# Two layers of a streaming encoder in fp32: the MLP's up projection as seven block products for eight, and the down projection as a stage of its own

## The chip, the cores and the metric

One core of a Trainium2 chip. The number that counts is the device time of one execution in microseconds (us), median of several runs. A kernel of this size shows runs that lie within about 0.3% of each other.

## What is computed

Two layers on 1152 tokens (1024 of a prompt, 8 x 16 new ones of running streams), all in fp32. In each layer three kinds of attention (MLA, gated linear attention, chunk band attention) add to `x` through `w_out`; then comes the MLP, which is all that the change touches:

```
def _mlp(h, w_up, w_down):
    return jnp.square(jax.nn.relu(h @ w_up)) @ w_down
# x = x + _mlp(_rmsnorm(x, norm2), w_up, w_down)
# x: 1152 x 1024, w_up: 1024 x 4096, w_down: 4096 x 1024
```

A last RMSNorm gives `y`.

## The kernel before

`x` is held transposed: eight tiles `xs[c]` of 128 channels (partitions) by 1152 tokens. Tokens go in three groups of `G` = 384, which is the width of a matmul's moving operand and of a PSUM bank's used part. The kernel lets a scheduler order the instructions of each engine; the priorities in the code (`tc.high_priority`) and the order of the code are its input.

**Products of high and low parts.** An fp32 operand is split in two fp32r tiles: the high part is a ScalarE copy to fp32r, the low part a VectorE (or GpSimd) subtraction of that copy from the source. A product is then three matmuls: high x high, high x low, low x high. `wsplit` does it for weights: one DMA of 512 KB into `raw`, one ScalarE copy of 128x1024 (L146), one VectorE subtraction of 128x1024 (L135, in the helper `sub_l`). `mm_step` (L209) issues the three matmuls of one contraction chunk, and all matmuls carry the line of the helper `mm`, L57.

**Ahead of the MLP.** `out_last` (L1190) adds the last part of the output projection to `x`: per chunk and group nine matmuls and one VectorE add (L1200, `x<-z,xo`). `norm_group` (L194) makes `h` of one group: `inv_rms` gives the reciprocal root mean square in PSUM (`rb`), then per chunk one VectorE product `hf` (L199), one ScalarE copy and one subtraction. All `h` of a layer, high and low, stays in SBUF (48 tiles of the pool `h`).

**The MLP.** It runs over 16 blocks `fb` of 256 hidden rows. `up(f)` makes 128 hidden rows for all three groups: 8 contraction chunks x 3 matmuls x 3 groups = 72 matmuls of 384 columns. `u_evac` squares: ScalarE relu (L1225) and square (L1226), GpSimd product (L1227), VectorE subtraction, so that `u` is in SBUF in high and low parts. `down(fb, us)` multiplies these two chunks with `w_down` and adds each of the 24 results to `xs` on VectorE (L1253, `x<-z,x`): 8 x 3 x 6 = 144 matmuls of 384 columns and 24 adds. So the code alternates:

```
for fb in range(16):
    if 0 < fb < 15:
        nxt = up(2 * fb + 2)
    (down if fb < 15 else down_last)(fb, us)
    if fb < 15:
        us = [nxt, up(2 * fb + 3)]
```

The first three chunks of `up` run group by group behind the norm (`behind_norm`), the last `down` group by group ahead of the next norm (`down_last`). A layer has 32 x 72 = 2304 matmuls of up and 16 x 144 = 2304 of down. `u` never leaves SBUF. All DMAs of the kernel are issued by SyncE (SP), in one order.

Of the kernel before, what the change touches and what calls it, by code (L numbers as in the profile page):

```python
# [9 lines left out]
F32 = mybir.dt.float32  # L10
# [6 lines left out]
P = 128  # L17
DEPTH = 2
# [8 lines left out]
N_STREAM = 8  # L27
LEVELS = (32, 16, 8, 4, 2, 1)
# [6 lines left out]
# in-projection chunks of 128 columns  # L35
# [4 lines left out]
def body(ctx, tc, t):  # L40
    nc = tc.nc
    cpool = ctx.enter_context(tc.tile_pool(name="const", bufs=1))
    hpool = ctx.enter_context(tc.tile_pool(name="h", bufs=48))
    ppool = ctx.enter_context(tc.tile_pool(name="piece", bufs=8))
    wpool = ctx.enter_context(tc.tile_pool(name="wts", bufs=3))
# [20 lines left out]
    # chunks whose squares, and whose sums of squares, GpSimd makes  # L66
# [30 lines left out]
    def banks(**bufs):  # L97
        """a new cut of the eight banks"""
# [57 lines left out]
    def inv_rms(srcs, width, scale=1.0, heads=1, pool=SQ_POOL):  # L156
        """1 / root mean square over the partitions (of each head) of the given [P, G] views, in PSUM"""
        pt = bank("nm" if "nm" in pcur else "tp", "ms")
        accs = {}
        for i, c in enumerate(srcs):  # L160
            q = ppool.tile([P, G], F32, tag="q", name=nm("sq"), bufs=4)
# [9 lines left out]
        for i, q in enumerate(accs.values()):  # L171
            for j in range(3):
                mm(pt[:, j * heads:(j + 1) * heads], q[:, j * P:(j + 1) * P], onec if heads == 1 else hsel,
                   start=i == 0 and j == 0, stop=i == len(accs) - 1 and j == 2)
        n = 3 * heads
        v, r, w = (sm("rr", 6, 12)[:, :n] for _ in range(3))
        V.tensor_scalar(v, pt[:, :n], scale / width, EPS * scale, ALU.mult, ALU.add)
# [6 lines left out]
        # one row of it for all partitions  # L184
        pr = bank("nm" if "nm" in pcur else "pv", "rb")
        m = P // heads
        for j in range(3):
            for h in range(heads):
                c = j * heads + h
                mm(pr[h * m:(h + 1) * m, j * P:(j + 1) * P], r[:, c:c + 1].to_broadcast([P, m]), ident,  # L190
                   start=True, stop=True)
        return pr[:, :G]
# [16 lines left out]
    def mm_step(outs, w, r, first, last_):  # L209
        """one contraction chunk of all groups in outs; w, r: (high, low)"""  # L210
# [33 lines left out]
    for l in range(DEPTH):  # L244
# [47 lines left out]
        def behind_norm(ws, put):  # L292
            """three columns of products over all chunks, group by group behind the norm"""
# [11 lines left out]
        def dense(o, w, r, n):  # L305
            """a bank over n contraction chunks"""
# [51 lines left out]
        def drive(primary, pc, fc):  # L358
            """merge the primary stream with the dense one, in proportion to their costs"""
# [35 lines left out]
        def attention(unit_iter, ap, wmax, ny, lag):  # L395
            """units of one head and two query tiles; a unit gives scores(a), j0(a), nk(a), v(j), out(ps)"""
# [23 lines left out]
            def t_step(u, a, pr):  # L420
                if a == 0:
# [6 lines left out]
                    # blocks that one of the two query tiles does not see  # L428
# [66 lines left out]
        def v_split(dst, src):  # L495
            """src [P, n, 128] two heads of values -> dst [P, n, 4, 64]: high|low, low|high"""
# [76 lines left out]
        def ca_setup2(c, ap, box):  # L573
# [15 lines left out]
            # sample: scores of this pair of heads  # L589
# [43 lines left out]
        def sample_pt(pnew, pc, pn, sc):  # L633
            """P^T of the cached keys [128, stream, 96] and of the new keys (own stream only)"""
# [774 lines left out]
```

## Time and profile before

| what | value |
|---|---|
| median of 3 runs | 3263.82 us (3259.57 to 3268.15) |
| the profiled execution: span from first to last instruction | 3266.2 us |
| TensorE (PE) busy | 3137.7 us, 96% |
| VectorE (DVE) busy | 1834.2 us, 56% |
| ScalarE (ACT) busy | 1190.6 us, 36% |
| GpSimd (POOL) busy | 866.1 us, 27% |
| DMA | 237.67 MB, mean 73 GB/s |
| MLP of the first layer, first up matmul to last | 828.6 us to about 1634 us |
| MLP of the second layer, last down matmul | about 3245 us |

The execution's time other than its span is not listed apart; its span lies 2.4 us over the median of the runs and inside their range. The page shows, for each engine, busy time, a strip of 40 slices of the span (a digit is the busy share in tenths; a slice is 81.7 us), the chain of work that ended last, the costliest groups of instructions with their mean duration, and DMA issues with their time to landing. PEld is the weight load that each matmul has; it overlaps the matmuls. Matmuls overlap too, so what one costs in a dense stretch is the distance between starts and not its duration.

### The profile page before, as it was taken

What the parts mean: (1) busy time and instruction counts of PE and PEld (TensorE: products, weight loads), DVE (VectorE), ACT (ScalarE), POOL (GpSimd) and SP (SyncE); (2) the same over time, 40 slices, a digit from 0 to 9 for tenths busy, and PEclk for the clock granted to TensorE, in tenths of its full rate; (3) what the DMA queues carried; (4) which work ended last, traced back from release to release, by engine and by line L of the source; (5) the groups of instructions that cost most, each with busy time, mean ns of one, the idle gap of its engine ahead of it and who ended that gap; (6) DMA issues with size and microseconds to landing.
All of it is one profiled execution on the core that took longest, in us unless ns stands there. A gap on an engine that the chain in (4) does not pass through costs nothing.

```text
span 3266.2 us, 49236 instructions
## 1 busy us (share of the span) xinstructions
PE 3137.7 (96%) x18652; PEld 2982.4 (91%) x18652; DVE 1834.2 (56%) x3785; ACT 1190.6 (36%) x2781; POOL 866.1 (27%) x1122
## 2 busy tenths in 40 slices
PE   8999998998999999999999999889999999999998
PEld 7888887887999999999989888878889999999998
DVE  4554687885734434434555646978855443434436
ACT  4443454774311121111244434557743121111122
POOL 5221355443310010100242214654532010010112
PEclk9999999989999999999999999999999999999998
DMA  5232215224011111111143222142331111111111
GB/s 182 86 100 78 88 50 159 67 83 149 30 43 46 39 46 40 46 39 46 62 140 105 85 74 86 57 150 75 111 104 39 46 40 46 40 46 45 40 46 59
DMA packets 137612, 237.67 MB, mean 73 GB/s; under 512 B 16768, under 2 KB 105056, under 8 KB 137376
## 3 DMA queue, kind: packets, MB, share of 16 engines
q1 hardware_dynamic: 137376, 234.53, 22.3%
q8 instruction: 147, 2.41, 0.3%
q14 instruction: 89, 0.73, 0.1%
HBM read 178.64 MB, written 55.84 MB: 72 GB/s over the span
## 4 chain that ended last, share of the span: by engine, by line
PE 82%; DVE 9%; ACT 4%; issue 3%; DMA 1%; POOL 1%; SPq 0%; DVEq 0%; ACTq 0%; POOLq 0%
PE z L57 67%; PE s L57 4%; PE pv L57 3%; PE ptp L72 2%; PE rb L57 1%; DVE ga L743 1%; PE glao L57 1%; DVE mq L734 1%; PE lev L57 1%; DVE sbd L796 1%; ACT P L413 1%; DVE M L729 1%; PE ms L57 0%; DVE ng L408 0%; ACT PT L151 0%
## 5 line engine op out<-in xcount | busy, mean ns | idle before, releaser
L57 PE MATMUL z<-u,wdnh 128*128 128x384 f32 x3072 | 712.9, 334 | 0.1
L57 PEld LDWEIGHTS z<-u,wdnh 128*128 128x128 f32 x3072 | 548.6, 188 | 0.4 <-DVE u L135 0.4
L1253 DVE TENSOR_TENSOR x<-z,x 128x384 f32<-128x384 f32 x720 | 364.5, 551 | 288.0 <-PE z L57 288.0
L1227 POOL TENSOR_TENSOR relu<-relu 128x384 f32<-128x384 f32 x192 | 166.7, 895 | 1340.8 <-ACT u L1226 1336.1
L57 PE MATMUL z<-u,wdnl 128*128 128x384 f32 x1536 | 445.9, 334 | 0.0
L57 PE MATMUL z<-hH,wupl 128*128 128x384 f32 x1536 | 373.3, 334 | 0.0
L57 PE MATMUL z<-hL,wuph 128*128 128x384 f32 x1536 | 373.1, 334 | 0.0
L57 PE MATMUL z<-hH,wuph 128*128 128x384 f32 x1536 | 372.2, 334 | 0.0
L146 ACT ACTIVATE wdnh<-wdnr 128x1024 fp32r<-128x1024 f32 x64 | 68.0, 1062 | 686.4 <-PE z L57 686.4
L57 PEld LDWEIGHTS z<-u,wdnl 128*128 128x128 f32 x1536 | 282.3, 188 | 0.0
L57 PEld LDWEIGHTS z<-hH,wupl 128*128 128x128 f32 x1536 | 275.8, 188 | 0.0
L57 PEld LDWEIGHTS z<-hL,wuph 128*128 128x128 f32 x1536 | 275.8, 188 | 0.0
L57 PEld LDWEIGHTS z<-hH,wuph 128*128 128x128 f32 x1536 | 275.7, 188 | 0.0
L146 ACT ACTIVATE wuph<-wupr 128x1024 fp32r<-128x1024 f32 x64 | 68.0, 1062 | 514.6 <-PE z L57 512.6
L135 DVE TENSOR_TENSOR wdnl<-wdnr,wdnh 128x1024 fp32r<-128x1024 f32 x64 | 78.1, 1221 | 302.7 <-ACT wdnh L146 302.7
L135 DVE TENSOR_TENSOR wupl<-wupr,wuph 128x1024 fp32r<-128x1024 f32 x64 | 78.2, 1221 | 205.8 <-ACT wuph L146 205.8
L413 ACT ACTIVATE P<-s,ng 128x320 f32<-128x320 f32 (+5 forms) x288 | 157.4, 552 | 85.8 <-DVE ng L410 59.1
L135 DVE TENSOR_TENSOR u<-relu,u 128x384 fp32r<-128x384 f32 x192 | 148.9, 801 | 50.9 <-POOL relu L1227 50.9
L135 DVE TENSOR_TENSOR PT<-ptp,PT 128x512 fp32r<-128x512 f32 (+3 forms) x288 | 146.0, 518 | 52.6 <-ACT PT L151 44.3
L151 ACT ACTIVATE PT<-ptp 128x512 fp32r<-128x512 f32 (+3 forms) x288 | 127.3, 460 | 126.1 <-PE ptp L72 116.5
L72 PE MATMUL ptp<-ident,P 128*128 128x128 f32 x792 | 139.9, 283 | 15.2 <-DVE PT L135 12.0
L408 DVE TENSOR_REDUCE ng<-s 128x1 f32<-128x320 f32 (+5 forms) x288 | 146.7, 516 | 7.0 <-PE s L57 2.7
(416 smaller groups left out, 6447.5 us busy)
## 6 DMA issues: line engine op xcount, KB each, us to landing
wupr<-in_w_up_dram SPq DMA_DIRECT2D x64, 512.0 KB, 3.3
wdnr<-in_w_down_dram SPq DMA_DIRECT2D x64, 512.0 KB, 3.3
zs_dram<-z SPq DMA_DIRECT2D x102, 192.0 KB, 1.9
wo1r<-in_w_out_dram SPq DMA_DIRECT2D x48, 320.0 KB, 3.0
of<-os_dram SPq DMA_DIRECT2D x48, 192.0 KB, 3.5
xpart_dram<-xo SPq DMA_DIRECT2D x48, 192.0 KB, 1.9
xo<-xpart_dram SPq DMA_DIRECT2D x48, 192.0 KB, 3.5
cf<-zs_dram SPq DMA_DIRECT2D x36, 192.0 KB, 4.3
```

The costliest lines, as they stand in the source:

```text
L57: i = T.matmul(*a, **k).ins
L72: T.transpose(out, in_, idn)
L135: eng.tensor_tensor(lo, src, h.bitcast(F32), ALU.subtract)
L146: S.activation(h, raw, AF.Copy)
L151: S.activation(o, i, AF.Copy, scale=scale)
L408: V.tensor_reduce(ng[:, x:x + 1], sc[x][:, :hi - lo], AX.X, ALU.max, negate=True)
L413: S.activation(pr[:, lo:hi], sc[x][:, :hi - lo], AF.Exp, bias=ng[:, 0:1], accum_out=ss[:, x:x + 1])
L729: V.tensor_tensor(mv[:, :, 0, :], mv[:, :, 0, :], kv[:, :, 0, :], ALU.mult)
L734: (GP if h else V).tensor_tensor(q2[hr, h, :w // 2].rearrange("p (n s) -> p n s", s=s), mv[hr, :, 1, :], qv[hr, :, 1, :], ALU.mult)
L743: V.copy_predicated(o, mk.to_broadcast([P, 2 * nt, 64 // s, s]), src)
L1227: GP.tensor_tensor(r, r, r, ALU.mult)
L1253: V.tensor_tensor(x[:, gsl(g)], o, x[:, gsl(g)], ALU.add)
```

## The change

Up and down become two stages, with `u` in DRAM between them.

**Up.** Both operands of up are cut in 2 x 2 blocks: the weights of a pair of hidden chunks (2 x 128 hidden rows, contraction in two halves of four chunks) and `f` = the normed `x` (contraction halves, token blocks of `Q` = 288; half `h` of the tokens is two such blocks). A block product then takes seven products in place of eight (Winograd's form of Strassen). `up_pair(i, halves)` does a pair: it loads 2 x 512 KB, forms four sums of weights (`ws`, two on GpSimd, two on VectorE, 128x512), splits seven operands (`oh` on ScalarE, `ol` on VectorE, 128x512), issues 7 x 4 x 3 = 84 matmuls of 288 columns for each half of the tokens, and combines the results: per half one ScalarE copy, five VectorE adds, then relu and square of four blocks, two on VectorE alone, two on ScalarE and GpSimd, and four stores to `u` in DRAM. `f_blocks` and `f_sums` make, per half, for each of four j: four VectorE products `f`, three VectorE and one GpSimd difference, then seven splits into tiles `hc` (ScalarE copy, VectorE subtraction, 128x288). The order of the code: norm and `hc` of half 0; pairs 0 to 3 for half 0 with norm and `hc` of half 1 in between; pairs 4 to 15 for both halves; pairs 0 to 3 for half 1, whose weights are loaded, summed and split a second time.

**Down.** Eight blocks of 512 hidden rows (2, 3, ..., 7, 0, 1). `load_u` reads four chunks of `u` (128x1152 each) and splits them, `load_d` loads and splits weights, and `down` runs 12 matmuls of 384 columns into one bank and adds the result to `x`: 24 adds a block, 192 a layer. In the first block the addend is `xo`, read from a copy `xmid` of `x` in DRAM, since `xs` is given up during up for the tiles `hc` of half 1.

**Pools.** `wts` and `h` are closed ahead of the MLP (`base.close()`) and opened again behind it, so their memory serves the MLP's pools.

The diff of the MLP, cut (comments and docstrings go too):

```diff
+Q = NT // 4
+KH = KD // 2
+PRODUCTS = range(7)
...
-        for g in range(NG):
-            with tc.high_priority(offset=100):
-                norm_group(xs, sml[:, SM_N2:SM_N2 + 8], hs, g)
...
-        def u_evac(u, g, o):
-            uh, ul = u[g]
-            r = piece("relu")
-            S.activation(r, o, AF.Relu)
-            S.activation(uh, r, AF.Square)
-            GP.tensor_tensor(r, r, r, ALU.mult)
-            sub_l(V, ul, r, uh)
...
-        def up(f):
-            w = wsplit(t["w_up"][l, f], [KD, P], "wup")
-            u = new_u()
-            outs = list(enumerate(dense3()))
-            for k in range(KD):
-                mm_step(outs, (w[0][:, k, :], w[1][:, k, :]), hs[k], k == 0, k == KD - 1)
-            for g, o in outs:
-                u_evac(u, g, o)
-            return u
...
-        def down(fb, us):
-            for half in range(2):
-                w = wsplit(t["w_down"][l, fb, half], [2, 512], "wdn")
-                for m in range(4):
-                    outs = list(enumerate(dense3()))
-                    for k in range(2):
-                        mm_step(outs, (w[0][:, k, m * P:(m + 1) * P], w[1][:, k, m * P:(m + 1) * P]), us[k],
-                                k == 0, k == 1)
-                    x = xs[half * 4 + m]
-                    for g, o in outs:
-                        V.tensor_tensor(x[:, gsl(g)], o, x[:, gsl(g)], ALU.add)
...
+        base.close()
...
+        hc = [[[mp.tile([P, 1, Q], F32R, name=nm("hc")) for _ in range(2)] for _ in range(KH)] for _ in PRODUCTS]
...
+        def f_sums(f):
+            f11, f12, f21, f22 = f
+            t1, t2, t3, t4 = (e_tile("t") for _ in range(4))
+            V.tensor_tensor(t1, f12, f11, ALU.subtract)
+            GP.tensor_tensor(t3, f22, f12, ALU.subtract)
+            V.tensor_tensor(t2, f22, t1, ALU.subtract)
+            V.tensor_tensor(t4, f21, t2, ALU.subtract)
+            return f11, t2, t3, t1, f21, t4, f22
...
+        def up_pair(i, halves):
...
+                r = mp.tile([P, KD, P], F32, tag="wr", name=nm("wur"), bufs=3)
+                load(r, t["w_up"][l, 2 * i + c])
...
+            GP.tensor_tensor(s1, a21, a22, ALU.add)
+            V.tensor_tensor(s2, s1, a11, ALU.subtract)
+            GP.tensor_tensor(s3, a11, a21, ALU.subtract)
+            V.tensor_tensor(s4, a12, s2, ALU.subtract)
...
+            def prod(n, src, banks_, first, after):
+                wh = mp.tile([P, KH, P], F32R, tag="oh", name=nm("oh"), bufs=5)
+                wl = mp.tile([P, KH, P], F32R, tag="ol", name=nm("ol"), bufs=5)
+                S.activation(wh, src, AF.Copy)
+                sub_l(V, wl, src, wh)
+                for h in halves:
...
+                    for j in range(KH):
+                        bh, bl = (x[:, 0, :] for x in hcs[h][n][j])
+                        for k, (w, r) in enumerate(((wh, bh), (wh, bl), (wl, bh))):
+                            mm(banks_[h], w[:, j, :], r, start=first and j == k == 0, stop=j == KH - 1 and k == 2,
...
+            def out(h, c, b, z, relu):
+                u = u_tile("u")
+                if relu:
+                    r = e_tile("r")
+                    S.activation(r, z, AF.Relu)
+                    GP.tensor_tensor(u, r, r, ALU.mult)
+                else:
+                    V.scalar_tensor_tensor(u, z, 0.0, z, ALU.max, ALU.mult)
+                store(t["u"][l, 2 * i + c, :, tsl(h, b)], u)
...
+            prod(0, a11, X, True, a1)
+            prod(1, s2, Y, True, a6)
+            prod(2, s3, Wb, True, a7)
+            prod(3, s1, Z, True, a5)
+            prod(4, a12, X, False, a2)
+            prod(5, a22, Wb, False, a4)
+            prod(6, s4, Z, False, a3)
...
+        up_pair(0, (0,))
+        rs = up_norm(1)
...
+        second([0], lambda: mp1)
+        up_pair(1, (0,))
+        second([1], lambda: mp1)
+        up_pair(2, (0,))
...
+        second([2, 3], last_pool)
+        up_pair(3, (0,))
+        banks(d=8)
+        for i in range(4, 16):
+            up_pair(i, (0, 1))
+        for i in range(4):
+            up_pair(i, (1,))
...
+        def load_u(n, b):
...
+                r = dp.tile([P, NT], F32, tag="ur", name=nm("ur"), bufs=2)
+                load(r, t["u"][l, 4 * b + q])
+                h, lo = (dp.tile([P, NT], F32R, tag=f"u{n % 2}", name=nm("u"), bufs=8) for _ in range(2))
+                copy(h, r)
+                sub_l(V, lo, r, h)
...
+        def down(us, ws, m, g, xo):
+            o = bank("d", "z")[:, :G]
+            c = slice((m % 4) * P, (m % 4 + 1) * P)
+            for q in range(4):
+                for k, (wi, ri) in enumerate(((0, 0), (0, 1), (1, 0))):
+                    mm(o, ws[q // 2][wi][:, q % 2, c], us[q][ri][:, gsl(g)], start=q == k == 0, stop=q == 3 and k == 2)
+            x = xs[m][:, gsl(g)]
+            V.tensor_tensor(x, o, x if xo is None else xo, ALU.add)
```

How the change moves instructions is shown at three places. The first is TensorE at the end of `out_last` in the first layer, before (`wo` and `oH`, `oL` are operands of the output projection, `hH`, `hL` the normed `x`, `wuph`, `wupl` the split weights):

```order
L57 MATMUL z_9274<-oH_9177,wo_8604 128x384
L57 MATMUL z_9274<-oL_9178,wo_8604 128x384
L57 MATMUL z_9274<-oH_9177,wo_8605 128x384
L57 MATMUL z_9597<-hH_9327,wuph_9563 128x384
L57 MATMUL z_9627<-hH_9327,wuph_9569 128x384
L57 MATMUL z_9657<-hH_9327,wuph_9575 128x384
L57 MATMUL z_9597<-hL_9328,wuph_9563 128x384
```

The same place after (`rb` is the second token block's reciprocal root mean square; `hc` a split operand of a product, `oh`, `ol` split weights):

```order
L58 MATMUL z_9274<-oH_9177,wo_8605 128x384
L58 MATMUL rb_9426<-ident,rr_9418 128x96 x3
L58 MATMUL z_9590<-hc_9290,oh_9586 128x288
L58 MATMUL z_9590<-hc_9291,oh_9586 128x288
L58 MATMUL z_9590<-hc_9290,ol_9587 128x288
L58 MATMUL z_9590<-hc_9292,oh_9586 128x288
L58 MATMUL z_9590<-hc_9293,oh_9586 128x288
L58 MATMUL z_9590<-hc_9292,ol_9587 128x288
L58 MATMUL z_9590<-hc_9294,oh_9586 128x288
L58 MATMUL z_9609<-hc_9298,oh_9605 128x288
```

The last matmul of `out_last` (`z_9274`) was followed by up products whose `hf` stood ahead of it on VectorE; now it is followed by block products, and their operands are made behind it, as the second place shows. That is VectorE at the same point, before:

```order
L199 SCALAR_TENSOR_TENSOR hf_9353<-x_8828,smalls_106,rb_9323 128x384
L1200 TENSOR_TENSOR x_8829<-z_9248,xo_9246 128x384
L181 SCALAR_TENSOR_TENSOR rr_9406<-rr_9404,rr_9405 128x3
L1200 TENSOR_TENSOR x_8830<-z_9261,xo_9259 128x384
L135 TENSOR_TENSOR hL_9334<-hf_9335,hH_9333 128x384
L199 SCALAR_TENSOR_TENSOR hf_9359<-x_8829,smalls_106,rb_9323 128x384
L135 TENSOR_TENSOR hL_9346<-hf_9347,hH_9345 128x384
L1200 TENSOR_TENSOR x_8831<-z_9274,xo_9272 128x384
```

And VectorE after:

```order
L1207 TENSOR_TENSOR x_8830<-z_9261,xo_9259 128x384
L1246 SCALAR_TENSOR_TENSOR f_9454<-x_8824,smalls_106,rb_9384 128x288
L1207 TENSOR_TENSOR x_8831<-z_9274,xo_9272 128x384
L1246 SCALAR_TENSOR_TENSOR f_9456<-x_8824,smalls_106,rb_9426 128x288
L1246 SCALAR_TENSOR_TENSOR f_9458<-x_8828,smalls_106,rb_9384 128x288
L1246 SCALAR_TENSOR_TENSOR f_9460<-x_8828,smalls_106,rb_9426 128x288
L1246 SCALAR_TENSOR_TENSOR f_9484<-x_8825,smalls_106,rb_9384 128x288
```

Six of the eight `hf` and two of the splits of the first group stood ahead of the add that ends `out_last` (`x_8831<-z_9274`); now one of the 16 `f` of half 0 does. The third place is SP's order at the end of up in the first layer. Before there is no such end; in the middle of the MLP the loads of both weights alternate, with nothing else between them:

```order
L141 DMA wupr_10479<-in_w_up_dram 128x1024
L141 DMA wupr_10581<-in_w_up_dram 128x1024
L141 DMA wdnr_10683<-in_w_down_dram 128x1024
L141 DMA wdnr_10785<-in_w_down_dram 128x1024
L141 DMA wupr_10887<-in_w_up_dram 128x1024
L141 DMA wupr_10989<-in_w_up_dram 128x1024
```

After, around the last store of `u` (`u_14349`, a result of the seventh product of the last pair):

```order
L76 DMA xo_14410<-xmid_dram 128x384
L76 DMA xo_14426<-xmid_dram 128x384
L76 DMA xo_14442<-xmid_dram 128x384
L79 DMA u_dram<-u_14349 128x288
L76 DMA xo_14458<-xmid_dram 128x384
L76 DMA xo_14474<-xmid_dram 128x384
L76 DMA xo_14490<-xmid_dram 128x384
L76 DMA ur_14374<-u_dram 128x1152
L76 DMA ur_14380<-u_dram 128x1152
L76 DMA wdr_14398<-in_w_down_dram 128x1024
L76 DMA wdr_14404<-in_w_down_dram 128x1024
```

All loads that the down stage begins with (`ur`, `wdr`) stand behind the store of the last result of up.

More of the change, by code (lines that the diff above doesn't have):

```diff
@@ new lines, in body, with tsl, u_tile, e_tile @@
+        mstack, tstack = ExitStack(), ExitStack()
+        mp = open_pool(mstack, "up")
+        hc = [[[mp.tile([P, 1, Q], F32R, name=nm("hc")) for _ in range(2)] for _ in range(KH)] for _ in PRODUCTS]
+        hcs = [hc, [[] for _ in PRODUCTS]]
+        gains = sml[:, SM_N2:SM_N2 + 8]
+        def tsl(h, b):
+            return slice((2 * h + b) * Q, (2 * h + b + 1) * Q)
+        def u_tile(s):
+            return mp.tile([P, Q], F32, tag="u", name=nm(s), bufs=8)
+        def e_tile(s):
+            return piece(s)[:, :Q]
@@ new lines, in f_blocks @@
+        def f_blocks(h, j, rs, into):
+            out = []
+            for c in (j, j + KH):
+                for b in range(2):
+                    x = xs[c][:, tsl(h, b)]
+                    f = x if into is None else into("f")
+                    V.scalar_tensor_tensor(f, x, gains[:, c:c + 1], rs[b], ALU.mult, ALU.mult)
+                    out.append(f)
+            return out
+        def f_sums(f):
[6 more added lines that the diff above has]
+            return f11, t2, t3, t1, f21, t4, f22
@@ new lines, in body, with second @@
+        with tc.high_priority(offset=100):
+            rs = up_norm(0)
+            for c in range(KD):
+                for g in range(NG):
+                    store(t["xmid"][:, c, gsl(g)], xs[c][:, gsl(g)])
+            for j in range(KH):
+                for i, f in enumerate(f_sums(f_blocks(0, j, rs, u_tile))):
+                    f_split(i, j, f, hcs[0][i][j])
+        up_pair(0, (0,))
+        rs = up_norm(1)
+        def second(js, pool):
+            fs = [f_blocks(1, j, rs, u_tile) for j in js]
+            pool = pool()
+            for j, f in zip(js, fs):
+                for i, f in enumerate(f_sums(f)):
+                    hcs[1][i].append([pool.tile([P, 1, Q], F32R, name=nm("hc")) for _ in range(2)])
+                    f_split(i, j, f, hcs[1][i][j])
@@ new lines, in body @@
+        dstack = ExitStack()
+        dp = open_pool(dstack, "down")
+        xpool = open_pool(xstack, "x", "right")
+        xs = [xpool.tile([P, NT], F32, name=nm("x")) for _ in range(KD)]
+        banks(d=6, nm=2)
+        def load_u(n, b):
+            us = []
+            for q in range(4):
[4 more added lines that the diff above has]
+                sub_l(V, lo, r, h)
+                us.append((h, lo))
+            return us
@@ new lines, in load_d @@
+        def load_d(b, half):
+            ws = []
+            for fb in (2 * b, 2 * b + 1):
+                r = dp.tile([P, 2, 512], F32, tag="wr", name=nm("wdr"), bufs=2)
+                load(r, t["w_down"][l, fb, half])
+                h, lo = (dp.tile([P, 2, 512], F32R, tag=f"w{x}", name=nm("wd"), bufs=5) for x in range(2))
+                S.activation(h, r, AF.Copy)
+                sub_l(V, lo, r, h)
+                ws.append((h, lo))
+            return ws
+        def down(us, ws, m, g, xo):
+            o = bank("d", "z")[:, :G]
+            c = slice((m % 4) * P, (m % 4 + 1) * P)
+            for q in range(4):
+                for k, (wi, ri) in enumerate(((0, 0), (0, 1), (1, 0))):
+                    mm(o, ws[q // 2][wi][:, q % 2, c], us[q][ri][:, gsl(g)], start=q == k == 0, stop=q == 3 and k == 2)
+            x = xs[m][:, gsl(g)]
+            V.tensor_tensor(x, o, x if xo is None else xo, ALU.add)
@@ new lines, in body @@
+        blocks = (2, 3, 4, 5, 6, 7, 0, 1)
+        for n, b in enumerate(blocks):
+            us = load_u(n, b)
+            if n < len(blocks) - 1:
+                for half in range(2):
+                    ws = load_d(b, half)
+                    for m in range(4 * half, 4 * half + 4):
+                        for g in range(NG):
+                            xo = None
+                            if n == 0:
+                                xo = piece("xo")
+                                load(xo, t["xmid"][:, m, gsl(g)])
+                            down(us, ws, m, g, xo)
+            else:
+                ws = [load_d(b, half) for half in range(2)]
+                for g in range(NG):
+                    for m in range(KD):
+                        down(us, ws[m // 4], m, g, None)
@@ L1296, in body @@
             nc.sync.dma_start(t["o_y"][:, c, gsl(g)], f)
+    base.close()
     xstack.close()
```

107 lines of the change are left out of this document (63 added, 44 removed).

## The prediction

> **What bounds the kernel now.** I read the page's engine shares and strips first, then the busy time by stretch inside the MLP, then single matmuls there.
>
> ```profile
> PE 3137.7 (96%) x18652; PEld 2982.4 (91%) x18652; DVE 1834.2 (56%) x3785; ACT 1190.6 (36%) x2781; POOL 866.1 (27%) x1122
> PE   8999998998999999999999999889999999999998
> DVE  4554687885734434434555646978855443434436
> PE 82%; DVE 9%; ACT 4%; issue 3%; DMA 1%; POOL 1%; SPq 0%; DVEq 0%; ACTq 0%; POOLq 0%
> ```
>
> TensorE is busy 96% of the span and holds 82% of the chain. The strips show two MLPs (slices 11 to 20 and 31 to 40) with TensorE full and VectorE at 3 to 5 tenths. By stretch (us, then busy time of PE, PEld, DVE, ACT, POOL, granted clock, DMA share, GB/s):
>
> ```profile
> 1250.00:1300.00 50.00, 50.00 (x291) 50.00 (x290) 21.07 (x34) 8.99 (x16) 5.11 (x6) 1.00 0.13 43
> 420.00:440.00 20.00, 15.21 (x113) 13.30 (x113) 19.42 (x51) 9.59 (x25) 9.10 (x13) 1.00 0.17 57
> 800.00:810.00 10.00, 7.95 (x45) 7.31 (x44) 4.70 (x10) 1.79 (x4) 2.15 (x3) 1.00 0.90 285
> 1640.00:1650.00 10.00, 9.05 (x46) 8.55 (x47) 6.83 (x10) 0.65 (x2) 4.70 (x3) 0.75 0.63 223
> ```
>
> The first row is mid-MLP: TensorE has no gap, at full clock, while VectorE idles for 29 of 50 us. So fewer matmul columns there are time won, if nothing else becomes late. The second is a stretch of gated attention where VectorE is busy 97% and TensorE 76%: such a stage goes at VectorE's pace. The third is the fastest DMA of the kernel, 285 GB/s at 90% of the engines. The fourth follows a gap in TensorE's work: its clock is granted at 0.75.
>
> What a matmul costs in a dense stretch is the distance of starts (start, us, count):
>
> ```profile
> 1300.34 0.68 PE L57 MATMUL z<-hH,wupl 128*128 128x384 f32 x3
> 1300.86 0.68 PE L57 MATMUL z<-hH,wuph 128*128 128x384 f32 x3
> 710.74 1.12 PE L57 MATMUL pv<-PT,mvhl 128*128 128x256 f32 x8
> 711.70 0.52 PE L57 MATMUL s<-k,qH 96*128 96x384 f32 x2
> ```
>
> Three of 384 columns take 0.52 us, 173.3 ns each; eight of 256 take 0.96 us, 120 ns each. Both are 13.3 ns over columns / 2.4 GHz, so 288 columns lie on the line between them at 133.3 ns (ends 120 and 173.3; the line is taken, since two rows with equal excess leave little else).
>
> **The matmuls.** Removed per layer: 2304 of 384 columns, 399.3 us. Added: 16 pairs x 2 halves x 84 = 2688 of 288, 358.3 us. Down keeps 2304 of 384 columns. TensorE's work falls by 41.0 us a layer, 82 us in all. The Trainium skill (TensorE: Matmul & The Clock Gate, "Back-to-back issue gap") gives columns / 2.4 GHz + 2.5 ns for a warm matmul. By that the saving would be 2304 x 162.5 - 2688 x 122.5 ns = 45.1 us a layer, 8 us more in all; the trace disagrees (173.3 against 162.5 ns), and its rows are used.
>
> **The start of up.** VectorE's prices, from rows:
>
> ```profile
> L135 DVE TENSOR_TENSOR wupl<-wupr,wuph 128x1024 fp32r<-128x1024 f32 x64 | 78.2, 1221 | 205.8 <-ACT wuph L146 205.8
> L1253 DVE TENSOR_TENSOR x<-z,x 128x384 f32<-128x384 f32 x720 | 364.5, 551 | 288.0 <-PE z L57 288.0
> 1271.08 1.49 DVE L1253 TENSOR_TENSOR x<-z,x 128x384 f32<-128x384 f32 x3 [0.97 <-PE z L57]
> 18.25 4.28 DVE L199 SCALAR_TENSOR_TENSOR hf<-x,smalls,rb 128x384 f32<-128x384 f32 x8
> L816 POOL TENSOR_TENSOR vx<-smask,ga 128x512 f32<-128x512 f32 x8 | 8.6, 1087 | 0.2
> L1227 POOL TENSOR_TENSOR relu<-relu 128x384 f32<-128x384 f32 x192 | 166.7, 895 | 1340.8 <-ACT u L1226 1336.1
> ```
>
> From 551 ns at 384 to 1221 at 1024 is 1.05 ns a column: 450 ns at 288, 685 at 512. Operations in a row overlap by some 0.08 us (three take 1.49 and not 1.65), which leaves 0.37 and 0.60 us; the products by scalar and `rb` (eight in 4.28, 0.53 each at 384) come to 0.43 at 288.
>
> Between the last add of `out_last` and the last split of half 1, VectorE's order holds 41 operations of 512 (weight sums and splits: 24.6 us), 105 of 288 (`hc` splits, `f` differences, result adds, squares: 38.9 us), 38 products of 288 (16.3 us) and some small ones (3 us): 83 us. Behind half 0 alone TensorE has pairs 0 to 3 (4 x 84 x 133.3 ns = 44.8 us) and most of pair 4's first half, 53 us. Ahead of it stands nothing: one `f` of 16 precedes the add that ends `out_last`. So TensorE idles at least 83 - 53 = 30 us in a layer.
>
> GpSimd adds to that. It has 10 sums of 512 (1.09 us each) and 23 operations of 288 (0.67 us each from 895 ns at 384), 26 us, and slows VectorE where both inputs of VectorE's operation are in SBUF:
>
> ```profile
> 1256.39 1.22 DVE L135 TENSOR_TENSOR wdnl<-wdnr,wdnh 128x1024 fp32r<-128x1024 f32 x1 [10.78 <-ACT wdnh L146]
> 1258.85 2.73 DVE L135 TENSOR_TENSOR u<-relu,u 128x384 fp32r<-128x384 f32 x3 [1.23 <-POOL relu L1227]
> 1257.99 2.71 POOL L1227 TENSOR_TENSOR relu<-relu 128x384 f32<-128x384 f32 x3 [35.04 <-ACT u L1226]
> 1270.47 2.40 POOL L1227 TENSOR_TENSOR relu<-relu 128x384 f32<-128x384 f32 x3 [9.77 <-ACT u L1226]
> 1273.67 0.54 DVE L135 TENSOR_TENSOR u<-relu,u 128x384 fp32r<-128x384 f32 x1
> ```
>
> Three such subtractions beside three GpSimd products took 2.73 us where they take 1.48 alone (0.54 + 2 x 0.47): 1.25 us lost in 1.85 us of overlap, 0.68. The three adds `x<-z,x` at 1271.08 us, with one input in PSUM, had GpSimd's products of 1270.47 us beside them and kept their pace. Of the 83 us, 57 are operations with two SBUF inputs (69%), so 26 x 0.68 x 0.69 = 12 us. At 97% busy, as at 420 us, another 3 us of waits for ScalarE's copies. The start costs 30 + 12 + 3 = 45 us a layer (29 if GpSimd is hidden, 58 if VectorE always yields). Before, this work hid under three up chunks; now its cover is gone.
>
> **Up's middle and end.** A pair of both halves needs 22.4 us of TensorE and 13 of VectorE (9 x 0.60 + 10 x 0.37 + 4 x 0.43, and 2 for GpSimd), and loads run two pairs ahead: nothing. Pairs 0 to 3 for half 1 have 11.2 us of TensorE against 8.1 + 1.6 us of VectorE: 1 us for the four (0 to 6).
>
> **DMA.** A layer writes `u` (32 x 128 x 1152 x 4 bytes, 18.9 MB), reads it again, loads 4.2 MB of weights twice, and writes and reads `xmid` (4.7 MB each): 51 MB in some 800 us, 64 GB/s over the 43 of mid-MLP and far from 285. SP issues about 420 DMAs more in both layers.
>
> ```profile
> L141 SPq DMA_DIRECT2D wdnr<-in_w_down_dram x64: 327/328/430, 750.2 to 3181.2; - x64
> ```
>
> At 0.33 us each that is 140 us of a queue that has 3266. I take nothing inside the stages; the cover is loads issued two pairs ahead, and if that went, each late load of 512 KB would cost its 3.3 us. What isn't covered is the joint between the stages.
>
> **From up to down.** The first `ur` load stands on SP behind the store of the last result.
>
> ```profile
> wdnr<-in_w_down_dram SPq DMA_DIRECT2D x64, 512.0 KB, 3.3
> L146 ACT ACTIVATE wdnh<-wdnr 128x1024 fp32r<-128x1024 f32 x64 | 68.0, 1062 | 686.4 <-PE z L57 686.4
> L1225 ACT ACTIVATE relu<-z 128x384 f32<-128x384 f32 x192 | 79.7, 482 | 12.8 <-PE z L57 12.3 <-DVE u L135 0.5
> ```
>
> From TensorE's last product: add, relu, square on GpSimd, about 1.8 us; then store, three `xo`, two `ur` of 590 KB and `wdr` of 512 KB, 2.4 MB, 8.6 us at 285 GB/s, before ScalarE can make the first weights (1.06 us): 11.5 us, and 1.5 us more while `ur` is refilled in two buffers. I take 13 us (8 if each load lands in 3.3 us as if alone; 18 with the clock lost after the gap). The adds that down saves on VectorE (384 to 192 a layer) free nothing that is waited for.
>
> **Between the layers.** The next layer's first weights now load behind `xspill` stores; TensorE already waits there (9.05 of 10 us at 0.75 clock). I add 3 us, once (0 to 8).
>
> **The sum.** Per layer -41 + 45 + 1 + 13 = +18; twice, and 3: +39 us on a span of 3266.2, 3305. That execution lies 2.4 us over the median of the runs, 3263.82, so 3303 against the runs. The ends of the terms give -41 + 29 + 0 + 8 = -4 a layer, 3256, and -41 + 58 + 6 + 18 = +41 and 8, 3354. About 0.3%, 10 us, is what can be told from no change.
>
> **Rivals.**
>
> *Faster: VectorE isn't the pace of the start.* The sum turns where start and reload together cost under 38 us a layer, 58 in my sum. If ScalarE's copies run well ahead, 288-wide operations cost no more than three quarters of 384-wide ones (0.35 us) and the scheduler's mix lets TensorE pass, the start costs 17 us; with 8 for the reload each layer gains 15 us: 3239. For it speaks that VectorE has the same kind of work before, hidden; against it the stretch at 420 us, and that 83 us of operations stand in one in-order queue ahead of half 1.
>
> *Same: only the floor.* GpSimd finds holes, the start costs 30 and the reload 8 us: 3260. For it: GpSimd's 26 us are little more than a quarter of the stage. Against: its sums and differences are what VectorE's next operations read, so both work in the same moments.
>
> *Slower still: the two share a port and one blocks.* VectorE waits for each whole GpSimd operation it meets, 18 us and not 12 of 26, and TensorE's clock falls in the holes:
>
> ```profile
> 1642.44 0.52 PE L57 MATMUL z<-hH,win10l 128*128 128x384 f32 x1
> 1642.76 0.52 PE L57 MATMUL z<-hH,win10h 128*128 128x384 f32 x1
> ```
>
> There 384 columns took 320 ns, so 288 would take 240, and 53 us of work 95: TensorE and VectorE then delay each other, some 10 us more a layer. 3303 + 2 x 16 = 3335. The Trainium skill (SBUF — State Buffer, "SBUF: two separate sides") says that the pair of ports is an exclusive lock, held for the whole instruction, against VectorE operations with two SBUF inputs. By that rule the loss is the 18 us; the trace's 0.68 is less than a full block.
>
> *The change doesn't save columns:* if 288 columns cost 384's 173.3 ns, up costs 66 us a layer more. The 256-column row excludes that.
>
> **How the numbers follow.** My forecast 62 in 100 (range 3256 to 3354; slower in 56 of them, same in 6); the floor 13 (same 8, faster 5); faster 15; slower still 10. Faster 20, same 14, slower 66. The range 3240 to 3350 leaves out half of the faster case and the far end of the slowest.
>
> **What would show it.** Right: in the profile after, up's matmuls are 133 ns apart in pairs 4 to 15; in the first some 95 us of up VectorE is busy over 90% and TensorE under 65%; TensorE's gap between the last `hc` and the first `wd` matmul is 10 to 18 us and ended by ScalarE's copy of a loaded tile. Wrong: a start with TensorE over 80%, or a gap of a few us, or holes in pairs 4 to 15, which I price at nothing and which would cost 268 us of TensorE work a layer its pace.

## The result, and the profile after

The changed kernel takes 3346.72 us (median; 3344.58 to 3348.83) where the kernel before, measured beside it, takes 3264.89 us (3259.57 to 3268.15): a ratio of 1.0248, with a 95% interval of 1.0236 to 1.026. The change makes the kernel 82 us slower. The forecast was 39 us slower, 3303 us; the direction and the range (3240 to 3350) held, the size did not.

The page after, with TensorE's total, its strip, VectorE's strip, the granted clock and the chain that ended last:

```profile
span 3342.7 us, 53103 instructions
PE 3107.8 (93%) x19456; PEld 2940.9 (88%) x19456; DVE 2029.7 (61%) x4185; ACT 1305.6 (39%) x2949; POOL 920.5 (28%) x1138
...
PE   8999998898699998999999999989886999899998
...
DVE  5554697885855565444445647968767555654444
...
PEclk9999999998799999999999999989887999999999
...
PE 59%; DVE 7%; DMA 2%; issue 2%; ACT 2%; POOL 1%; SPq 0%; DVEq 0%; POOLq 0%; ACTq 0%
```

TensorE is busy 30 us less than before, and its span is 76.5 us longer: it now has holes. The deepest stand in slices 10 and 11 (and 30 and 31 in the second layer; 84 us each), with 6 to 8 tenths, where the granted clock sinks too: the start of up. By stretch (us, then busy time and instructions of PE, PEld, DVE, ACT, POOL, the granted clock, DMA share, GB/s), first the time from the end of the output projection to VectorE's last split of half 1, then mid-up, the last four pairs, and the joint:

```profile
817.45:926.40 108.95, 67.73 (x357) 61.65 (x356) 92.95 (x193) 48.42 (x113) 50.25 (x33) 0.72 0.22 73
940.00:960.00 20.00, 20.00 (x153) 20.00 (x152) 10.62 (x20) 6.11 (x12) 4.20 (x6) 1.00 0.28 90
1205.00:1230.00 25.00, 24.22 (x182) 23.98 (x182) 21.06 (x33) 10.04 (x20) 8.39 (x8) 1.00 0.36 118
1230.00:1255.00 25.00, 18.09 (x114) 17.62 (x112) 11.70 (x20) 5.46 (x11) 5.45 (x6) 0.86 0.24 78
1255.00:1280.00 25.00, 14.84 (x76) 14.84 (x77) 13.67 (x13) 11.73 (x11) 0.00 (x0) 0.73 0.88 302
```

Mid-up is full, as mid-MLP was before, and a matmul of 288 columns costs what the forecast took. The timeline there (start, us, count), twelve starts in 1.58 us:

```profile
950.04 0.43 PE L58 MATMUL z<-hc,oh 128*128 128x288 f32 x2
950.30 0.29 PE L58 MATMUL z<-hc,ol 128*128 128x288 f32 x1
...
951.62 0.43 PE L58 MATMUL z<-hc,oh 128*128 128x288 f32 x2
```

Over all of pairs 4 to 15, 2016 matmuls take 268.0 us, 132.9 ns each. With that, the time that TensorE loses in up can be counted: the time from the end of the output projection's last matmul to the start of the up matmul with the number in the first column, less 132.9 ns for each of up's matmuls so far.

| up's matmuls so far | layer 1: us since, of it lost | layer 2: us since, of it lost |
|---|---|---|
| 84 (pair 0, half 0) | 38.3, 27.2 | 36.6, 25.5 |
| 168 | 58.2, 35.9 | 58.2, 35.9 |
| 252 | 80.0, 46.5 | 80.8, 47.3 |
| 336 (pairs 0 to 3, half 0) | 113.7, 69.0 | 114.4, 69.7 |
| 2352 (pairs 4 to 15) | 381.7, 69.0 | 382.3, 69.7 |
| 2688 (pairs 0 to 3, half 1) | 433.1, 75.8 | 429.9, 72.6 |

The start costs 69 us a layer, where the forecast had 45. From the end of the output projection to down's last matmul a layer takes 852.3 and 849.6 us, where it took 805.3 and 804.8: 46 us more, forecast 18. That is 92 us for both. The rest of the program is 15 us shorter in this execution, 11 of it in the first layer's attention; profiled executions of the kernels below, which have the same program up to there, end that attention anywhere between 817 and 827 us, so a difference of some 10 us there is within the scatter (the medians differ by 82).

### The profile page after: what moved, and what is told of

It reads as the page before. It is cut to its first block, busy times and chain, and to the rows that moved or that the text cites. A ratio compares the mean times of both kernels' runs of the same rounds, so it can differ in the third digit from the quotient of the medians.

```text
span 3342.7 us, 53103 instructions
## 1 busy us (share of the span) xinstructions
PE 3107.8 (93%) x19456; PEld 2940.9 (88%) x19456; DVE 2029.7 (61%) x4185; ACT 1305.6 (39%) x2949; POOL 920.5 (28%) x1138
## 4 chain that ended last, share of the span: by engine, by line
PE 59%; DVE 7%; DMA 2%; issue 2%; ACT 2%; POOL 1%; SPq 0%; DVEq 0%; POOLq 0%; ACTq 0%
PE z L58 51%; PE s L58 2%; PE pv L58 2%; PE ptp L73 1%; DMA wur<-in_w_up_dram 1%; DVE ol L140 1%; POOL t L1255 0%; DMA wdr<-in_w_down_dram 0%; PE rb L58 0%; DVE ga L750 0%; DVE mq L741 0%; PE glao L58 0%; DVE hc L140 0%; DVE f L1246 0%; DVE sbd L803 0%
## 5 line engine op out<-in xcount | busy, mean ns | idle before, releaser
L58 PE MATMUL z<-u,wd 128*128 128x384 f32 x4608 | 807.6, 336 | 27.5 <-ACT wd L1406 27.5
L58 PEld LDWEIGHTS z<-u,wd 128*128 128x128 f32 x4608 | 802.6, 189 | 28.0 <-ACT wd L1406 28.0
L58 PE MATMUL z<-hc,oh 128*128 128x288 f32 x3584 | 753.3, 306 | 78.6 <-DVE ec L1309 27.0
L58 PEld LDWEIGHTS z<-hc,oh 128*128 128x128 f32 x3584 | 602.6, 197 | 88.8 <-ACT r L1301 27.4
L58 PE MATMUL z<-hc,ol 128*128 128x288 f32 x1792 | 544.9, 305 | 8.5 <-DVE ol L140 8.5
L1418 DVE TENSOR_TENSOR x<-z,x 128x384 f32<-128x384 f32 x336 | 186.3, 555 | 324.4 <-PE z L58 324.1
L58 PEld LDWEIGHTS z<-hc,ol 128*128 128x128 f32 x1792 | 351.9, 197 | 11.6 <-DVE ol L140 11.2
L1285 ACT ACTIVATE oh<-ws 128x512 fp32r<-128x512 f32 x160 | 99.5, 630 | 263.0 <-PE z L58 225.4
L1302 POOL TENSOR_TENSOR u<-r 128x288 f32<-128x288 f32 x128 | 92.0, 719 | 370.4 <-ACT r L1301 246.0
L140 DVE TENSOR_TENSOR ol<-ws,oh 128x512 fp32r<-128x512 f32 x160 | 110.1, 692 | 61.8 <-ACT oh L1285 61.6
```

The lines of the kernel that those rows point to most:

```text
L58: i = T.matmul(*a, **k).ins
L140: eng.tensor_tensor(lo, src, h.bitcast(F32), ALU.subtract)
L1285: S.activation(wh, src, AF.Copy)
L1302: GP.tensor_tensor(u, r, r, ALU.mult)
L1418: V.tensor_tensor(x, o, x if xo is None else xo, ALU.add)
```

## What was tried on the chip

Two theories stood for the 24 us a layer that the forecast had missed in the start. A: VectorE's queue paces it, and the slow clock follows from TensorE's holes. B: the slow clock is itself the missing term. From the end of the output projection to matmul 336, TensorE runs 65 us at half clock in the first layer; its holes add up to 41 us, and the other 28 of the 69 are put down to matmuls at half speed.

**e_cold and e_warm: idle work that holds the clock up.** The control has one bank less; e_warm uses that bank for matmuls that nobody reads:

```
-        banks(d=6, nm=2)
+        banks(d=5, nm=2, dm=1)          # e_cold: banks(d=5, nm=2)
...
             sub_l(V, dst[1][:, 0, :], f, dst[0][:, 0, :])
+            d = bank("dm", "dummy")[:, :Q]
+            for _ in range(n):           # 3 for half 0, 6 for half 1
+                mm(d, dst[0][:, 0, 0:P], dst[0][:, 0, :], start=True, stop=True)
```

> The changed kernel with 5 result banks instead of 6 in the start of up (the control of e_warm; nothing else differs). Both theories: within 8 us of the changed kernel's 3347 us; the loss of TensorE up to the end of pair 3 stays at 65 to 75 us a layer.

> As e_cold, and TensorE is given idle work in the start of up: behind each split of a block of the normalized input, 3 (half 0) or 6 (half 1) matmuls of 288 columns into a bank that nobody reads, 252 in a layer, 34 us at full clock, of which most falls into holes. Theory A (VectorE's queue paces the start, the slow clock only follows from TensorE's holes): the half-clock time falls from 65 us to under 30 a layer, and yet the time stays within 15 us of e_cold, since the last split of half 1 comes when it came before. Theory B (the half clock is the term that the forecast left out: 28 of the 69 us lost are matmuls at half speed): 40 to 56 us faster than e_cold, some 3295 us.

e_cold took 3351.79 us (3349.10 to 3353.76), e_warm 3359.07 (3352.51 to 3364.90). The windows from the end of the output projection to the first matmul of pair 4, e_cold first:

```profile
822.90:935.91 113.01, 69.42 (x379) 64.10 (x378) 94.02 (x197) 49.16 (x115) 48.02 (x33) 0.71 0.22 74
```

```profile
820.50:939.43 118.93, 98.70 (x632) 90.89 (x631) 98.03 (x199) 49.68 (x116) 49.80 (x34) 0.89 0.24 77
```

The mean clock rises from 0.71 to 0.89 and the half-clock time up to VectorE's last split falls from 62 to 24 us a layer, but that split comes 109.6 and 108.0 us after the output projection, where it comes after 107.8 and 109.7 in e_cold. Nothing is won; the last idle matmuls even delay pair 4 by 4 us. The idle matmuls are 34 us of TensorE's work a layer themselves, so e_warm alone could hide a small gain. But VectorE is busy for 93.0 of the 109.0 us in the changed kernel: whatever TensorE's clock is, the stretch could not get shorter by more than the 16 us that VectorE idles, and most of these waits are for ScalarE (list further down). Theory B, 20 to 28 us a layer, falls. The Trainium skill (TensorE: Matmul & The Clock Gate, "HAM oscillation — how this bites in real kernels") has as its rule to leave TensorE no idle gaps over some 3.4 us, so that its clock stays up; here filling the gaps raises the clock and not the speed.

**e_nolow: 28 operations of VectorE less.**

```
-                sub_l(V, wl, src, wh)
+                if halves == (0,):
+                    wl = wh
+                else:
+                    sub_l(V, wl, src, wh)
```

> Leaves out the low parts of the weights in pairs 0 to 3 for half 0 (the high part is used in their place, so TensorE has as many matmuls): 28 VectorE subtractions of 512 columns less in a layer, nothing else. Theory A: VectorE's 28 x 0.65 us = 18 us are won in each layer, 36 in all, some 3310 us. Theory B: VectorE has no part in it beyond the waits, at most 10 us in all, 3337 us or more.

3323.63 us (3311.65 to 3327.80), 23 us less. The time lost in the start falls from 69 to 52 and 54 us a layer, 16 on average, where theory A said 18. The time lies between the theories: 36 us less by A, at most 10 by B. (By the profiles the two MLPs are 35 us shorter together, and the first attention, which ended at 827 us here, 10 us longer: the scatter named above.) The window up to pair 4 is 17 us shorter than the changed kernel's, which stands first, and VectorE's busy time in it is 17 us less too:

```profile
817.45:931.28 113.83, 72.61 (x379) 66.53 (x378) 95.33 (x197) 49.05 (x114) 50.25 (x33) 0.72 0.22 73
827.09:923.76 96.67, 61.05 (x378) 56.67 (x378) 78.38 (x169) 48.39 (x114) 41.52 (x33) 0.81 0.26 86
```

What VectorE is spared here, the stage is spared, one for one.

**e_nonorm1: half 1's normalization left out.** `second` and `up_norm(1)` go, and `hcs[1]` holds half 0's blocks:

```
-        rs = up_norm(1)
...
+        for n in range(7):
+            hcs[1][n].extend(hcs[0][n])
```

> Leaves out the normalization, sums and splits of half 1 (its products read half 0's blocks, so TensorE has as many matmuls): 27 us of VectorE, 28 copies on ScalarE and 4 sums on GpSimd less in a layer. Theory A: at least VectorE's 27 us are won in each layer, 3293 us, and up to the 42 us that TensorE loses behind pair 0 if its waits for the adds in VectorE's queue go too, 3263 us; what is left of the loss (27 to 42 us) lies in pair 0, where half 0 is normalized. Theory B: the holes of pair 0 keep the clock at half as long as now, so that at most 20 us a layer go, 3307 us.

3265.09 us (3251.82 to 3269.01), 82 us less: a layer's MLP is at 804.7 and 805.3 us, what it took before the change. The loss in the start is 28 us, of which 25.6 and 23.4 lie in pair 0, where half 0 is normalized; pairs 1 to 3 lose 3 to 5 us together. Half 1's normalization thus costs 41 us, though VectorE's busy time up to pair 4 falls by only 31 us (95.3 to 64.6); its copies on ScalarE and its squares and differences on GpSimd go with it. How it becomes TensorE's time, the changed kernel's own trace shows. This is the end of pair 3, TensorE and VectorE (start, us; in brackets the idle time before and what ended it):

```profile
911.99 0.29 PE L58 MATMUL z<-hc,ol 128*128 128x288 f32 x1
912.02 3.05 DVE L1246 SCALAR_TENSOR_TENSOR f<-x,smalls,rb 128x288 f32<-128x288 f32 x7
...
924.50 0.45 DVE L1309 TENSOR_TENSOR eb<-z,ea 128x288 f32<-128x288 f32 x1
...
925.24 0.45 DVE L1309 TENSOR_TENSOR ec<-z,eb 128x288 f32<-128x288 f32 x1
...
925.83 0.82 PE L58 MATMUL z<-hc,oh 128*128 128x288 f32 x2 [13.55 <-DVE ec L1309]
```

Products 4 to 6 of a pair go on adding in the banks of products 0, 2 and 3, from which the first results must have been read before: by ScalarE's copy `ea`, and by VectorE's adds `ec` (which needs `eb`) and `z`. Those adds stand in VectorE's in-order queue behind half 1's `f`, differences and splits, from 912.02 us on. TensorE has no other work that it may start, since its queue is in order too, and stands for 13.55 us.

**e_nogp: GpSimd's sums left out of the start.**

```
+            t3 = f12
-            GP.tensor_tensor(t3, f22, f12, ALU.subtract)
...
+            if halves == (0,):
+                s1, s3 = a21, a11
+            else:
                 GP.tensor_tensor(s1, a21, a22, ALU.add)
                 GP.tensor_tensor(s3, a11, a21, ALU.subtract)
```

> The changed kernel without GpSimd's sums in the start of up: in pairs 0 to 3 for half 0 two weight blocks stand in for the two sums of GpSimd, and a block of the input for GpSimd's difference (8 operations of 512 and 8 of 288 columns less in a layer, on GpSimd alone; VectorE has as many as before). Forecast's term (GpSimd takes 12 us from VectorE through what the two share): the loss in the start falls by 10 to 14 us a layer, 3347 - 24 = 3323 us. Rival (VectorE yields for whole operations of GpSimd, and waits for its sums): 15 to 20 us a layer, some 3310 us. Other rival (GpSimd's work is beside and takes nothing): 3340 us or more.

3321.04 us (3317.62 to 3335.99), 26 us less; the start loses 57 and 58 us a layer, 12 less. That is inside the 10 to 14 us of the forecast's term. But the forecast's 12 us were for all of GpSimd's work in the start, and this kernel leaves out its sums alone (33 operations become 17); nor is it all time that GpSimd takes from VectorE's operations, as the same stretch shows (to VectorE's last split; without GpSimd's sums it takes 96.87 us and not 108.95):

```profile
823.43:920.30 96.87, 62.66 (x357) 56.39 (x356) 87.95 (x193) 48.49 (x113) 16.36 (x17) 0.77 0.25 82
```

VectorE's busy time falls by 5 us, from 92.95 to 87.95; the other 7 are idle time, 16.0 before and 8.9 now. VectorE's waits for copies `hc`, 4.5 us in the changed kernel, are gone; ScalarE there waits 14.1 us for GpSimd's differences before it can make them. How an operation of VectorE gets longer, the groups of one of them (line, engine, operation, shapes, count, busy us, mean ns, idle before; the changed kernel, then e_nogp) and three rows of the changed kernel's timeline show:

```profile
L1257 DVE TENSOR_TENSOR t<-f,t 128x288 f32<-128x288 f32 x8 | 5.2, 654 | 0.0
```

```profile
L1257 DVE TENSOR_TENSOR t<-f,t 128x288 f32<-128x288 f32 x8 | 3.6, 447 | 0.0
```

```profile
840.05 4.44 POOL L1255 TENSOR_TENSOR t<-f,f 128x288 f32<-128x288 f32 x1 [6.90 <-ACT oh L1285]
848.48 1.36 POOL L1278 TENSOR_TENSOR ws<-wur,wur 128x512 f32<-128x512 f32 x1 [2.76 <-issue]
848.64 1.52 DVE L1257 TENSOR_TENSOR t<-f,t 128x288 f32<-128x288 f32 x1
```

The mean of 654 ns is six operations at 0.44 us and two that met one of GpSimd's: the one at 848.64 us ended 0.32 us after GpSimd's sum did. In the first layer's start 21 operations of VectorE took over 0.1 us longer than the shortest of their kind, 11.0 us together (18 operations and 9.3 us in the second layer). Every one of them began beside an operation of GpSimd and ended at the same distance behind one's end: 0.31 to 0.32 us with 288 columns, 0.54 to 0.55 us with 512, 0.02 us with the one of 3. So VectorE waited for the whole operation. It goes the other way too: the GpSimd difference at 840.05 us took 4.44 us, where the shortest of its kind takes 0.79, while VectorE ran operation after operation.

**e_joint: down's first loads ahead.** Half 0's blocks become 14 tiles of 1152 columns in a pool that stays open through down; the first block's `u`, its splits and the first two `wdr` take their room before up's pool is closed (down's other `ur`, `wdr` and half of its `u` take turns in these tiles too):

```
+        hp0 = open_pool(hstack, "up0")
+        def hu(s): return hp0.tile([P, NT], F32R, tag="hu", name=nm(s), bufs=14)
...
+        us0 = load_u(0, blocks[0])
+        raw0 = raw_d(blocks[0], 0)
         tstack.close()
         mstack.close()
```

> The changed kernel with down's first block of u and its first two weight tiles loaded ahead, into the room of half 0's blocks, which nobody reads in up's last four pairs. Theory of the joint (its 14 us are loads that wait on SP behind the last store of u and then land, with the slow clock after it 16): the gap falls to some 3 us, 12 us a layer, 3347 - 24 = 3323 us. Rival (the splits of that block, 8 of 1152 columns on VectorE and ScalarE, now delay up's last four pairs, and the second weight tiles still wait): 4 us a layer or less, 3339 us or more.

3318.85 us (3314.62 to 3326.60), 28 us less. The joint of the changed kernel on SP and TensorE, and then TensorE's in e_joint:

```profile
1252.67 0.32 SPq L79 DMA_DIRECT2D u_dram<-u  x1
1253.09 1.35 SPq L76 DMA_DIRECT2D xo<-xmid_dram  x3
1254.53 0.86 SPq L76 DMA_DIRECT2D ur<-u_dram  x2
1255.48 1.17 SPq L76 DMA_DIRECT2D wdr<-in_w_down_dram  x2
...
1265.16 3.25 PE L58 MATMUL z<-u,wd 128*128 128x384 f32 x9 [14.35 <-ACT wd L1406]
```

```profile
1258.11 1.33 PE L58 MATMUL z<-u,wd 128*128 128x384 f32 x3 [5.75 <-ACT wd L1409]
```

TensorE's gap falls from 14.35 to 5.75 us (13.17 to 6.17 in the second layer), 8 us a layer and not the 11 or 12 expected. The rest of the 28 is not settled: by the profiles a layer's MLP is 15 and 6 us shorter. In the first layer the last four pairs lost 2 us and not 7, and the start 3 us less.

**x_plain: pairs 0 to 4 without Strassen for half 0.**

```
+        def plain_pair(i):
...
+            for c in range(2):
+                z = [bank("d", "z")[:, :Q] for _ in range(2)]
+                for y in range(2):
...
+                    S.activation(wh, raw[c][:, y * KH:(y + 1) * KH, :], AF.Copy)
+                    sub_l(V, wl, raw[c][:, y * KH:(y + 1) * KH, :], wh)
+                    for j in range(KH):
+                        for b in range(2):
+                            bh, bl = (x[:, 0, :] for x in plain[j][2 * y + b])
+                            for k, (w, r) in enumerate(((wh, bh), (wh, bl), (wl, bh))):
+                                mm(z[b], w[:, j, :], r, ...)
```

Besides, these pairs square on ScalarE and VectorE, without GpSimd, `u` has four buffers in place of eight and `oh` and `ol` four in place of five, for room, and down's blocks go in the order 3, 4, ..., 7, 0, 1, 2. Half 0's differences and their splits (`sums0`) and all of half 1 (`second`) are recorded between these pairs; the rest of up is as it was, with pairs 0 to 4 for half 1 at the end.

> Pairs 0 to 4 are computed for half 0 as 8 plain block products (96 matmuls of 288 for 84), which need neither the 4 sums of weights nor the adds of results, and of half 0 only the 4 blocks themselves; half 0's sums and all of half 1's are made beside them. Theory A (what VectorE must do before and between TensorE's products sets the start): before the first product VectorE has 16 products and 16 splits (some 13 us), and a plain pair needs some 5 us of it for 12.8 of TensorE's, so that half 1's 27 us and half 0's other 11 fit beside 64 us. The loss in the start falls from 69 to some 20 us a layer, the 60 matmuls more cost 8: 3347 - 2 x 41 = 3265 us (3245 to 3290). Rival (the loss is in the latency from copy to split to product, one tile behind the other, and in GpSimd's sums): the loss stays at 45 us or more, 3315 us or more.

3266.27 us (3261.48 to 3272.82), 80 us less, won by all of this together. The loss up to matmul 576, in pair 5, is 21.8 and 21.4 us a layer. The window up to pair 5's first matmul:

```profile
817.99:902.14 84.15, 73.19 (x522) 71.99 (x522) 71.19 (x167) 43.97 (x112) 19.36 (x17) 0.92 0.37 117
```

**x_plainj: x_plain and e_joint together.**

> x_plain and e_joint together. If the two terms are independent, as the forecast's sum takes them: the time of x_plain less what e_joint gains on the changed kernel, some 3265 - 24 = 3241 us. Rival (less loss in the start leaves up's end as the tight place, with VectorE at work on block 2 of u): 3255 us or more.

3236.82 us (3235.68 to 3238.13). The two gains, 80 and 28 us, add up to 3238, so the two terms are independent within 2 us. The gap at the joint is 2.03 us.

**x_plainj6: six plain pairs.** `range(5)` becomes `range(6)` for the plain pairs and for half 1's pairs at the end.

> x_plainj with 6 plain pairs in place of 5. Theory A: the hole of 5.6 us at the change from plain pairs to the others (VectorE's rest of half 1) goes, with the slow clock after it, since a further plain pair brings 12.8 us of TensorE's work for 5 of VectorE's; 12 matmuls more cost 1.6 us: 5 to 6 us a layer, 3237 - 11 = 3226 us. Rival (the hole stands at that place whatever comes ahead, from the new result banks there): 3237 + 3 = 3240 us.

3224.79 us (3222.49 to 3236.56), a ratio of 0.9884 to the kernel before (0.9862 to 0.9906), which took 3264.85 us beside it. Its interval lies below 1: it is 1.2% faster than the kernel before. The profile is of the longest of its four executions, 3236.56 us. From its page, its start (to the first matmul of pair 6), a hole in the last pairs, and the joint:

```profile
PE 3090.6 (96%) x19600; PEld 2930.5 (91%) x19600; DVE 1998.1 (62%) x4133; ACT 1298.3 (40%) x2961; POOL 873.5 (27%) x1098
...
PEclk9999999899999999999999999999999999999999
```

```profile
825.93:915.77 89.84, 85.05 (x620) 83.82 (x619) 75.33 (x177) 47.88 (x123) 23.67 (x17) 0.94 0.40 130
```

```profile
1158.25 1.37 PE L58 MATMUL z<-hc,oh 128*128 128x288 f32 x4 [5.46 <-ACT oh L1292]
1218.94 21.27 PE L58 MATMUL z<-u,wd 128*128 128x384 f32 x121 [2.03 <-ACT wd L1451]
```

TensorE is busy 85 of the first 90 us of up, and the start loses 13 us a layer up to matmul 577, 7 less than x_plainj up to there. The hole at the change of banks falls from 5.7 to 0.8 us, and with it the rival, by which it would have stayed. What this version still loses lies at the other end: 10 and 8 us in the last pairs, most of it in one hole of 5.46 us (4.3 in the second layer) in the second of them. It ends a chain of late work: GpSimd's sum waited for up's weights, VectorE's for GpSimd's, ScalarE's copy for VectorE's, and TensorE for that copy. No run tried to mend it.

## Why the forecast was right in direction and half the size

- **Matmul columns: right.** 132.9 ns for 288 columns (forecast 133.3), so up's work falls by 42 us a layer (forecast 41).
- **Start of up, 45 us: this is the step that failed; it measured 69.** Its working was 98 us of VectorE less 53 us of TensorE work beside it. VectorE's last split came after 109.0 us: 93.0 busy (82 of its own and 11 waiting inside operations for GpSimd, where 83 and 12 had been counted, so that part was right), and 16.0 idle, where "another 3 us of waits for ScalarE's copies" stood. The waits of VectorE in that stretch (us in total, times, longest):

```profile
DVE ol L140 <- ACT oh L1285: 5.1, 5, 1.8
DVE hc L140 <- ACT hc L156: 4.5, 4, 1.2
DVE rr L184 <- PE ms L58: 2.4, 1, 2.4
DVE z L1309 <- PE z L58: 2.3, 3, 1.4
DVE ws L1277 <- POOL ws L1276: 1.2, 1, 1.2
DVE x L1207 <- PE z L58: 0.6, 1, 0.6
```

  So VectorE ended 11 us late. And "Behind half 0 alone TensorE has pairs 0 to 3 [...] and most of pair 4's first half, 53 us" was wrong: by that moment it had started 315 matmuls, 42 us of work, in both layers. That number is 312 to 315 in e_cold, e_warm, e_nolow and e_nogp too, whenever the moment came: TensorE's last products of pair 3 wait for adds that VectorE gives only after half 1's normalization. And of pair 4 there are, in the code's order, only 12 matmuls to take, since `prod` runs each product for both halves in turn and the next 12 read half 1's blocks: so the cover was at most 46 us and not 53, and the waits left 42. 11 + 11 us, and 2 more at half clock to the end of pair 3, are the missing 24. The forecast had set two engines side by side that hand work to each other in both directions, each through an in-order queue.
- **GpSimd, 12 us: right in size.** VectorE's operations lost 11.0 and 9.3 us a layer beside GpSimd's. That e_nogp wins 12 as well is in part chance: it leaves out the sums alone, which cost 5 us inside VectorE's operations and 7 in waits that stand nowhere in this term.
- **The 0.68 was misread.** In the row of the kernel before that the prediction shows (1258.85 us), the two longer subtractions ended 0.41 us after the GpSimd product beside them: they, too, had waited for the whole operation, as the slower-still rival said. Its 18 us did not come, since GpSimd in turn waits for VectorE; the 12 came out near the measured 11 by another way than the one that was taken.
- **The slower-still rival's clock** had the sign of the miss without being its cause: 65 us at half clock, and e_warm, with 24, took no less time.
- **Pairs 4 to 15, nothing: right** (loss 69.0 us ahead of them and behind them).
- **Last four pairs, 1 us: 6.8 and 2.9.** Up's weights come late there. SP and GpSimd at the worst place:

```profile
1221.68 3.94 SPq L79 DMA_DIRECT2D u_dram<-u  x3
1226.26 0.33 SPq L76 DMA_DIRECT2D wur<-in_w_up_dram  x1
```

```profile
1231.87 1.28 POOL L1276 TENSOR_TENSOR ws<-wur 128x512 f32<-128x512 f32 x1 [5.01 <-DMA wur<-in_w_up_dram]
```

  The last pair's load was issued behind three stores of `u`, and GpSimd had its weights 5.6 us after that. VectorE waited 3.84 us for GpSimd's sum, the add that frees a bank stood behind it in VectorE's queue, and TensorE stood for 2.73 us. The pairs are half as long there, so three `wur` buffers reach less far ahead. Whether the order on SP or the number of buffers does it was not tried.
- **Joint, 13 us: right**, 14.35 and 13.17, ended by ScalarE's copy of a loaded tile, as said. The clock stays at half 3.5 and 5.3 us into down, which costs another 2 or 3, inside the range given (8 to 18).
- **Between the layers, 3 us: not seen**; the second layer's attention took 805.6 us, where it took 806.3.
- **What would show it:** TensorE under 65% in the start held (67.73 of 108.95 us, 62%), VectorE over 90% did not (85%): that was the sign of the waits.

Per layer, as measured: -42 + 69 + 5 + 14, and 6 us lost in down (2 or 3 of them to the slow clock) less the 6.5 that the kernel before loses at its own ends, give the 46.

## What to carry to other kernels

When an algorithm trades matmuls for element-wise work, price the moment at which that work has no cover: here 42 us of TensorE were won by a change whose preparation and joint cost 88. Set two engines' work side by side only after following the waits in both directions; an add that frees a bank, queued behind someone else's preparation, stops TensorE as surely as a missing operand. The remedy was to do the first few pairs in the plain way, which needs the least preparation, and to prepare the clever way behind them: 8 us more of matmuls took 48 us off the loss.

## What the runs showed of the chip

VectorE and GpSimd wait for each other by whole operations, as told under e_nogp: where a VectorE operation with its inputs in SBUF lost time to one of GpSimd, it ended 0.32 us (288 columns) or 0.55 us (512) after GpSimd's had ended, and a GpSimd difference of 0.79 us took up to 5.97 us beside VectorE operations in a row, which lost nothing. What decides which of the two waits was not looked into.

The clock falls without one long gap. In the start of the first layer TensorE was granted the full clock from 841.98 to 845.39 us, and then half of it for 10.24 us. The windows ahead of the fall, at full clock and behind the fall, and the longest gap since 830 us:

```profile
830.00:845.39 15.39, 11.92 (x43) 9.68 (x43) 14.23 (x34) 8.46 (x23) 6.84 (x3) 0.61 0.20 68
841.98:845.39 3.41, 1.76 (x11) 1.34 (x10) 2.25 (x7) 0.87 (x3) 3.41 (x2) 1.00 0.55 197
845.39:855.63 10.24, 8.76 (x33) 7.94 (x33) 9.73 (x18) 5.23 (x11) 4.84 (x6) 0.50 0.01 2
```

```profile
845.02 0.40 PE L58 MATMUL z<-hc,oh 128*128 128x288 f32 x1 [1.65 <-ACT hc L156]
```

The Trainium skill (TensorE: Matmul & The Clock Gate, "HAM oscillation — how this bites in real kernels") has as its rule that gaps over some 3.4 us cost the clock; here none was over 1.65 us in the 15 us ahead of the fall (1.27 us at the same place in the second layer). And a higher clock need not save time: e_warm's start ran at 0.89 in place of 0.71 and took no less.
